# Recurrence chain of a two-layer hybrid decoder step: inverses joined in two column groups, samples and values two at a time, decay folded into the state's rows on GpSimd, fewer operations in VectorE's queue

## The chip, the cores and the metric

The kernel runs on one core of one Trainium2 chip. A core has TensorE (PE in the profile, its weight loads PEld), VectorE (DVE), ScalarE (ACT), GpSimd (POOL), and SyncE (SP), which issues most transfers. The metric is the device time of one execution in microseconds (us); lower is better.

## The reference

One inference step of two layers for a prompt of 512 tokens and 8 decoding samples of one token each, model width 2048. Each layer normalises and modulates its input, multiplies it by one wide matrix, sends one part of the columns through windowed attention (16 heads) and the other through RWKV-7 time mixing (16 heads of 64), gates both, and multiplies by an output matrix. The change touches only the time mixing, whose recurrence is, for each head:

```python
def step(S, inp):
    r_t, w_t, k_t, v_t, kk_t, a_t = inp
    sa = jnp.einsum('bhij,bhj->bhi', S, -kk_t)
    S = (S * w_t[:, :, None, :] + sa[..., None] * (kk_t * a_t)[:, :, None, :]
         + v_t[..., None] * k_t[:, :, None, :])
    return S, jnp.einsum('bhij,bhj->bhi', S, r_t)
```

The 512 prompt tokens start from S = 0, the 8 samples take one step each from a given state.

## The kernel before

**Layout and the large products.** Channels lie on the 128 partitions, the 520 columns (512 tokens and 8 samples) along the free axis. Every product of the input or output matrix is done as three fp32r matmuls per 128x128 block, from a high and a low part of weights and of activations (`quarter`, L370 to L385: `psP`, `psR`, `psQ`, `psA`, `psO` by kind of column tile, 128x260 each). ScalarE makes the high part of a weight block (`hi`, L353), VectorE the low part (`lo`, L363), three blocks ahead of its use.

**Interleaving.** The order on every queue is the order in which the program emits instructions. After each of those large matmuls `Side.tick` runs at most one step of one of the side generators, each of which says with `yield W[n]` how many matmuls are to pass before its next step. So the small work of the recurrence stands in TensorE's queue between large matmuls, at distances that `W` fixes, and in VectorE's, ScalarE's and GpSimd's queues in the same order of emission. Engines work their queues in order; a buffer or a result that is late stops the queue that needs it.

**The chain of one pair of heads.** `chain(p, ...)` (L533 to L842) handles two heads; there are 8 pairs in a layer, 16 in all, and the chain of one pair overlaps with the start of the next. The 512 tokens are cut into 8 chunks of 64, in two groups `g` of four. In order:

- `qk`, `kb` (L603 to L619): queries and keys times decay factors, by VectorE. `rkh` and `rks` (L622, L645; tiles `xhi`, `xlo`) are the two parts of r*k for the bonus term; `bp` (L650) sums them on TensorE.
- `atp` (L634) are the products kb by qk of a chunk; VectorE masks them into `atk` and `atq` (L638), and SyncE writes parts of `atk` to memory (`d1`).
- GpSimd reads them back as `f` (L655) and inverts 32 triangular blocks of 32x32 in 31 steps (L663, L665) into `xi`. During these steps TensorE turns `kb` (`kbT`, L671) and the values (`vT`, L687), ScalarE copies them to `kbt` and to the upper half of `sv`, and `av` (L696) is computed and copied by VectorE to the lower half of `sv` (L701).
- `xi` goes through memory (`d2`) into `xT` (L713), whose unused parts VectorE (L710) and GpSimd (L711) set to zero.
- Two inverses of 32 make one of 64: VectorE turns blocks into `x1` (L721), TensorE multiplies (`t2a`, L726), VectorE copies (L728), TensorE multiplies again (L732), VectorE copies into `xT` (L734). This is done for `g` = 0 and then `g` = 1, 8 products each.
- Eight chunks in sequence (tile `seq`): `rp` (L752) from the state `m0` (tiles `mbd`), `rr` (L753) on VectorE, `sp` (L761), `sv` (L762, L763) on VectorE, `mn` and `yp` (L765 to L768), and the new state by VectorE (L772), which multiplies `mn` by the chunk's decay `pend8` and adds `mp`, the decayed old state made at L756.
- The samples (L785 to L812): `st`, `sa`, `vz` on VectorE, `sab` (L800, L801) on TensorE, then `ys` (L810), one product for each sample, and its copies (L812).

GpSimd also copies the samples' columns (`smp`, L599) early in each chain. Small PSUM tiles come from a ring of four (`ps1`), 128-partition work tiles from a ring of 71 (`t2`). The lines that set the order around the change:

```python
if item[0] <= self.count:
    self.last = self.count
    self.run(item)
```

Of the kernel before, what the change touches and what calls it, by code (L numbers as in the profile page):

```python
# [9 lines left out]
F32 = mybir.dt.float32  # L10
F32R = mybir.dt.float32r
AF = mybir.ActivationFunctionType
ALU = mybir.AluOpType
# [158 lines left out]
def body(ctx, tc, xt, ct, consts, pars, wada, win, wout, lora, sst, swkv, ck, cv, cvn, fing,  # L172
# [324 lines left out]
    def layer(l, hh, hl, xprev, xnext, start, prepare, after):  # L497
# [35 lines left out]
        def chain(p, lw, r, kr, v):  # L533
# [89 lines left out]

            atq, atk = [], []
# [20 lines left out]
            rks = low(rk, rkh)  # L645
# [7 lines left out]
            f = wk.tile([128, 32, 32], F32, tag="inv", name="f", bufs=1)  # L653
            for j in range(4):
                ge.dma_start(out=f[j:128:4], in_=d1.rearrange("b c s t -> (b c) s t"))  # L655
# [5 lines left out]
            for s in range(31):  # L661
# [20 lines left out]
                if s in (15, 25):  # L682
                    g = (s - 5) // 10 - 1
                    ps = ps1("vT").rearrange("p (x t) -> p x t", t=128)
                    for e in range(4):
                        c = 4 * g + e
                        pe.transpose(ps[0:64, e, :], v[:, 64 * c:64 * c + 64], ident)  # L687
                    b = t2([128, 4, 128], "sv")
                    se.copy(out=b[0:64], in_=ps[0:64])
                    sv.append(b)  # L690
                if s == 30:
# [6 lines left out]
                    for g in range(2):  # L698
                        for h in range(2):
                            hs = slice(64 * h, 64 * h + 64)  # L700
                            ve.tensor_copy(sv[g][64:128, :, hs], ps[hs, 4 * g:4 * g + 4])  # L701
                yield W[25] if s < 20 else W[74]
            yield W[26]
            d2 = dp.tile([2, 16, 32, 32], F32, tag="d2", name="d2")
            ge.dma_start(out=d2.rearrange("b c (j i) t -> (b c j) i t", j=4), in_=xi)
            yield W[27]
            xT = []
            for g in range(2):
                a = t2([128, 4, 2, 64], "xT")
                ve.memset(a[0:64], 0.0)  # L710
                ge.memset(a[96:128, :, :, 0:32], 0.0)  # L711
                for b in range(2):
                    ge.dma_start(out=flat(a)[64 + 32 * b:96 + 32 * b, :, 32 * b:32 * b + 32],  # L713
                                 in_=d2[b, 8 * g:8 * g + 8].rearrange("c j t -> j c t"))
                xT.append(a)
            yield W[28]

            x1s, pas = [], []
            for g in range(2):
                x1s.append(sm.tile([128, 8, 32], F32, tag="x1", name="x1", bufs=2))  # L720
                ve.transpose(out=x1s[g][64:96], in_=flat(xT[g])[64:96, :, 0:32])  # L721
            yield W[29]
            for g in range(2):
                pas.append(ps1("t2a").rearrange("p (x t) -> p x t", t=32))
                for e in range(8):
                    pe.matmul(pas[g][96:128, e, :], flat(atk[g])[64:96, e, 32:64], x1s[g][64:96, e, :],  # L726
                              start=True, stop=True)
                ve.tensor_copy(x1s[g][96:128], pas[g][96:128, 0:8])  # L728
                yield W[30]
            for g in range(2):  # L730
                for e in range(8):
                    pe.matmul(pas[g][64:96, 8 + e, :], x1s[g][96:128, e, :], flat(xT[g])[96:128, e, 32:64],  # L732
                              start=True, stop=True)
# [750 lines left out]
```

## Time and profile before

| What | us |
|---|---|
| median of 3 runs | 2412.47 (2407.11 to 2414.36) |
| the profiled execution's own time | 2411.21 |
| its span, first to last instruction | 2409.4 |
| TensorE busy in the span | 2267.3 (94%) |
| VectorE busy | 1540.2 (64%) |
| ScalarE busy | 1031.0 (43%) |
| GpSimd busy | 727.8 (30%) |

The span lies 1.8 us below the profiled execution's own time. In the lines below, a row of instructions has its place in the program, engine, operation, tiles (written before read), shape and count; then busy time in us and the mean duration of one in ns; then how long the engine stood idle just before them and what released it. The view in order of time gives the start and the length in us. The records show an fp32 matmul of the small kind as two records (two passes), a transpose and an fp32r matmul as one. The granted TensorE clock was 0.979 of full speed over the span.

### The profile page before, as it was taken

Reading aid. Unit: us, or ns where it says so; the run is one execution under the profiler, and the core shown is the slowest. Engines: PE = TensorE matmul, PEld = TensorE weight load, DVE = VectorE, ACT = ScalarE, POOL = GpSimd, SP = SyncE. Lnnn points to the kernel's source line nnn. Section 1 sums busy time; section 2 is a strip of 40 time slices with the busy share of each in tenths; the row PEclk is TensorE's granted clock in tenths of the full one; section 3 lists DMA queues with packets and bytes.
Section 4 is the critical chain, followed back from the end, with each engine's and each line's share of the span. In section 5 each row is a group of like instructions: output and inputs, shape, how many; then the busy total and the mean of one; then the engine's idle time right before and its main releaser. Section 6 shows DMA issues by size and latency. Waiting matters only on the chain. (4 is left out here: it accounts for less than half of the span.)

```text
span 2409.4 us, 54300 instructions
## 1 busy us (share of the span) xinstructions
PE 2267.3 (94%) x20900; PEld 2125.9 (88%) x20900; DVE 1540.2 (64%) x3888; ACT 1031.0 (43%) x2250; POOL 727.8 (30%) x1348
## 2 busy tenths in 40 slices
PE   5999999999999999999999999998999999999997
PEld 3899988888889888889989999988989898889997
DVE  3465677777777687543356557677677777865445
ACT  3243344544454456422235335343544445653222
POOL 1106445654366000000012425654565530000112
PEclk8999999999999999999999999999999999999998
DMA  9945555323323224677773455543223332245345
GB/s 343 342 154 173 152 150 159 92 82 94 98 88 90 65 77 127 201 234 248 241 228 88 126 160 167 164 124 98 80 89 94 94 91 63 67 116 148 109 119 176
DMA packets 231396, 338.02 MB, mean 140 GB/s; under 512 B 61761, under 2 KB 82369, under 8 KB 230977
## 3 DMA queue, kind: packets, MB, share of 16 engines
q1 hardware_dynamic: 225248, 321.95, 44.3%
q0 software_dynamic: 5888, 12.59, 1.7%
q8 instruction: 165, 2.70, 0.5%
q14 instruction: 95, 0.77, 0.1%
HBM read 303.97 MB, written 32.56 MB: 140 GB/s over the span
## 5 line engine op out<-in xcount | busy, mean ns | idle before, releaser
L363 DVE TENSOR_TENSOR lo<-raw,hi 128x512 fp32r<-128x512 f32 x568 | 405.2, 714 | 441.1 <-PE psO L378 132.2
L353 ACT CAST hi<-raw 128x512 fp32r<-128x512 f32 x568 | 350.6, 618 | 633.7 <-PE psP L378 219.9
L378 PE MATMUL psP<-hh,hi 128*128 128x260 f32 x1408 | 306.3, 292 | 0.2 <-ACT dm L516 0.2
L378 PE MATMUL psP<-hh,lo 128*128 128x260 f32 x1408 | 306.4, 292 | 0.0
L378 PE MATMUL psP<-hl,hi 128*128 128x260 f32 x1408 | 305.8, 292 | 0.0
L663 POOL TENSOR_TENSOR tmp<-f,xi 128x248 f32<-128x248 f32 (+30 forms) x496 | 260.1, 524 | 81.6 <-DMA f<-d 44.2
L665 POOL TENSOR_TENSOR xi<-xi,tmp 128x248 f32<-128x248 f32 (+30 forms) x496 | 264.0, 532 | 38.9
L378 PEld LDWEIGHTS psP<-hh,hi 128*128 128x128 f32 x1408 | 224.2, 191 | 5.8 <-issue 2.9
L378 PEld LDWEIGHTS psP<-hh,lo 128*128 128x128 f32 x1408 | 224.4, 191 | 5.5 <-issue 3.7
L378 PEld LDWEIGHTS psP<-hl,hi 128*128 128x128 f32 x1408 | 224.5, 191 | 4.6 <-issue 2.5
L378 PE MATMUL psO<-yh,hi 128*128 128x260 f32 x1024 | 223.6, 284 | 3.6 <-DVE xsn L1182 3.6
L378 PE MATMUL psO<-yh,lo 128*128 128x260 f32 x1024 | 223.9, 284 | 1.8 <-DVE lo L363 1.8
L378 PE MATMUL psO<-yl,hi 128*128 128x260 f32 x1024 | 223.4, 284 | 0.0
L378 PEld LDWEIGHTS psO<-yh,hi 128*128 128x128 f32 x1024 | 165.3, 190 | 5.7 <-issue 5.6
L378 PEld LDWEIGHTS psO<-yh,lo 128*128 128x128 f32 x1024 | 165.9, 190 | 3.6 <-DVE lo L363 2.0
L378 PEld LDWEIGHTS psO<-yl,hi 128*128 128x128 f32 x1024 | 165.2, 190 | 1.6 <-issue 1.6
L779 ACT COPY y<-seq 64x64 f32<-64x64 f32 x256 | 52.9, 207 | 262.7 <-DVE mbd L772 215.0
L1319 POOL TENSOR_SCALAR yo<-xnew,fg 128x260 f32<-128x260 f32 x32 | 32.1, 1006 | 404.1 <-DVE xnew L1179 384.4
L443 POOL TENSOR_TENSOR rmsr<-rmsv,mhalf 128x3 f32<-128x3 f32 x6 | 5.6, 940 | 488.4 <-DVE rmsv L440 459.4
L297 PE MATMUL adps<-rawa,cT 128*32 128x128 f32 (+1 forms) x2048 | 116.5, 347 | 26.3 <-DMA rawa<-in_wada_dram 26.1
L378 PE MATMUL psQ<-hl,hi 128*128 128x260 f32 x512 | 116.5, 298 | 0.0
L378 PE MATMUL psQ<-hh,lo 128*128 128x260 f32 x512 | 116.1, 298 | 0.0
(361 smaller groups left out, 5499.5 us busy)
## 6 DMA issues: line engine op xcount, KB each, us to landing
raw<-in_win_dram SPq DMA_DIRECT2D x424, 256.0 KB, 3.3
rawa<-in_wada_dram SPq DMA_DIRECT2D x384, 256.0 KB, 4.8
raw<-in_wout_dram SPq DMA_DIRECT2D x152, 256.0 KB, 3.4
f<-d POOLq DMA_DIRECT2D x64, 128.0 KB, 3.1
gd<-th SPq DMA_DIRECT2D x22, 260.0 KB, 2.3
gr<-gd SPq DMA_DIRECT2D x22, 260.0 KB, 3.7
x<-in_xt_dram SPq DMA_DIRECT2D x16, 260.0 KB, 5.1
yd<-rk SPq DMA_DIRECT2D x16, 260.0 KB, 3.4
```

What stands on the lines that cost most here:

```text
L297: pe.matmul(ap[32 * g:32 * g + 32, 0:w], cT[:, kk, :], raw[g * w // 512][:, c:c + w], start=(kk == 0), stop=(kk == KT - 1))
L353: se.copy(out=his[n], in_=raws[n])
L363: ve.tensor_tensor(out=lo, in0=raws.pop(n), in1=hi, op=ALU.subtract)
L378: pe.matmul(ps[:, h, 0:NH], a[:, k % 4], b[:, h * NH:(h + 1) * NH], start=(k == k0 and j == 0), stop=stop)
L443: ge.tensor_tensor(out=r[:, 0:3], in0=v[:, 0:3], in1=mhalf[:, 0:3], op=ALU.pow)
L663: ge.tensor_tensor(out=tv, in0=f[:, s:s + 1, s + 1:32].to_broadcast([128, 8, 31 - s]), in1=xi[:, :, s:s + 1].to_broadcast([128, 8, 31 - s] ...
L665: ge.tensor_tensor(out=xi[:, :, s + 1:32], in0=xi[:, :, s + 1:32], in1=tv, op=ALU.add)
L779: se.copy(out=y[hs, 64 * c:64 * c + 64], in_=yp[hs, h])
L1319: ge.tensor_scalar(out=out[h][m // 2][:, m % 2], in0=xn[:, h * NH:h * NH + NH], scalar1=fg[:, m:m + 1], scalar2=None, op0=ALU.mult)
```

## The change

Line numbers of the diff are those of the file before; the changed file's numbers are higher by 2 to 9.

```diff
--- before.py
+++ after.py
@@ -621,6 +621,8 @@
             bc = lambda ap: ap.unsqueeze(2).to_broadcast([128, B, 64])
             rkh = high(rk)
 
+            yield W[23] // 2
+            rks = low(rk, rkh)
             atq, atk = [], []
             flat = lambda ap: ap.rearrange("p e h t -> p (e h) t")
             d1 = dp.tile([2, 16, 32, 32], F32, tag="d1", name="d1")
@@ -642,7 +644,6 @@
                 for b in range(2):
                     sy.dma_start(out=d1[b, 8 * g:8 * g + 8].rearrange("c s t -> s c t"),
                                  in_=flat(atk[g])[64 + 32 * b:96 + 32 * b, :, 32 * b:32 * b + 32])
-            rks = low(rk, rkh)
             yield W[23]
             b2 = rk
             for h in range(2):
@@ -651,6 +652,10 @@
                 yield W[24]
 
             f = wk.tile([128, 32, 32], F32, tag="inv", name="f", bufs=1)
+            for g in range(2):
+                b = kb[g].rearrange("p e a t -> p e (a t)")
+                ge.tensor_tensor(out=b, in0=b, in1=pend8[:, 4 * g:4 * g + 4].unsqueeze(2).to_broadcast([128, 4, 128]),
+                                 op=ALU.mult)
             for j in range(4):
                 ge.dma_start(out=f[j:128:4], in_=d1.rearrange("b c s t -> (b c) s t"))
             xi = wk.tile([128, 8, 32], F32, tag="xi", name="xi", bufs=1)
@@ -682,11 +687,12 @@
                 if s in (15, 25):
                     g = (s - 5) // 10 - 1
                     ps = ps1("vT").rearrange("p (x t) -> p x t", t=128)
-                    for e in range(4):
-                        c = 4 * g + e
-                        pe.transpose(ps[0:64, e, :], v[:, 64 * c:64 * c + 64], ident)
+                    for e in range(2):
+                        c = 4 * g + 2 * e
+                        pe.transpose(ps[:, e, :], v[:, 64 * c:64 * c + 128], ident)
                     b = t2([128, 4, 128], "sv")
-                    se.copy(out=b[0:64], in_=ps[0:64])
+                    for e in range(2):
+                        se.copy(out=b[0:64, e:4:2], in_=ps[64 * e:64 * e + 64, 0:2])
                     sv.append(b)
                 if s == 30:
                     ps = ps1("av").rearrange("p (c i) -> p c i", i=64)
@@ -698,41 +704,44 @@
                     for g in range(2):
                         for h in range(2):
                             hs = slice(64 * h, 64 * h + 64)
-                            ve.tensor_copy(sv[g][64:128, :, hs], ps[hs, 4 * g:4 * g + 4])
+                            se.copy(out=sv[g][64:128, :, hs], in_=ps[hs, 4 * g:4 * g + 4])
                 yield W[25] if s < 20 else W[74]
             yield W[26]
+            xT = [t2([128, 4, 2, 64], "xT") for _ in range(2)]
             d2 = dp.tile([2, 16, 32, 32], F32, tag="d2", name="d2")
             ge.dma_start(out=d2.rearrange("b c (j i) t -> (b c j) i t", j=4), in_=xi)
             yield W[27]
-            xT = []
-            for g in range(2):
-                a = t2([128, 4, 2, 64], "xT")
-                ve.memset(a[0:64], 0.0)
+            for a in xT:
+                ge.memset(a[0:64], 0.0)
                 ge.memset(a[96:128, :, :, 0:32], 0.0)
+            for g, a in enumerate(xT):
                 for b in range(2):
                     ge.dma_start(out=flat(a)[64 + 32 * b:96 + 32 * b, :, 32 * b:32 * b + 32],
                                  in_=d2[b, 8 * g:8 * g + 8].rearrange("c j t -> j c t"))
-                xT.append(a)
             yield W[28]
 
-            x1s, pas = [], []
-            for g in range(2):
-                x1s.append(sm.tile([128, 8, 32], F32, tag="x1", name="x1", bufs=2))
-                ve.transpose(out=x1s[g][64:96], in_=flat(xT[g])[64:96, :, 0:32])
+            x1 = sm.tile([128, 2, 8, 32], F32, tag="x1", name="x1", bufs=1)
+            for i in range(2):
+                ve.transpose(out=x1[64:96, i], in_=flat(xT[i])[64:96, :, 0:32])
             yield W[29]
-            for g in range(2):
-                pas.append(ps1("t2a").rearrange("p (x t) -> p x t", t=32))
-                for e in range(8):
-                    pe.matmul(pas[g][96:128, e, :], flat(atk[g])[64:96, e, 32:64], x1s[g][64:96, e, :],
-                              start=True, stop=True)
-                ve.tensor_copy(x1s[g][96:128], pas[g][96:128, 0:8])
-                yield W[30]
-            for g in range(2):
-                for e in range(8):
-                    pe.matmul(pas[g][64:96, 8 + e, :], x1s[g][96:128, e, :], flat(xT[g])[96:128, e, 32:64],
-                              start=True, stop=True)
-                ve.tensor_copy(flat(xT[g])[64:96, :, 32:64], pas[g][64:96, 8:16])
-                yield W[31]
+            pa = ps1("t2a").rearrange("p (x t) -> p x t", t=32)
+            for e in range(8):
+                for i in range(2):
+                    o = (96, 64)[i]
+                    pe.matmul(pa[o:o + 32, e, :], flat(atk[i])[64:96, e, 32:64], x1[64:96, i, e, :], start=True, stop=True)
+            for i in range(2):
+                o = (96, 64)[i]
+                ve.tensor_copy(x1[96:128, i], pa[o:o + 32, 0:8])
+            yield W[30]
+            for e in range(8):
+                for i in range(2):
+                    o = (64, 96)[i]
+                    pe.matmul(pa[o:o + 32, 8 + e, :], x1[96:128, i, e, :], flat(xT[i])[96:128, e, 32:64], start=True,
+                              stop=True)
+            for i in range(2):
+                o = (64, 96)[i]
+                ve.tensor_copy(flat(xT[i])[64:96, :, 32:64], pa[o:o + 32, 8:16])
+            yield W[31]
             y = t2([128, N], "y")
             for c in range(8):
                 if c == 6:
@@ -752,8 +761,6 @@
                     pe.matmul(rp, qk[g][:, e].rearrange("p a t -> p (a t)"), m0, start=True, stop=True)
                     ve.tensor_tensor(out=rr[64:128], in0=rp[64:128], in1=sv[g][64:128, e], op=ALU.add)
                     yield W[32] + 4
-                    mp = sm.tile([128, 128], F32, tag="mp", name="mp", bufs=2)
-                    ve.tensor_scalar(out=mp, in0=m0, scalar1=pend8[:, c:c + 1], scalar2=None, op0=ALU.mult)
                 else:
                     ve.tensor_copy(rr[64:128], sv[g][64:128, e])
                     yield W[32] + 4
@@ -769,11 +776,10 @@
                 for h in range(2):
                     hs = slice(64 * h, 64 * h + 64)
                     if c:
-                        ve.scalar_tensor_tensor(out=m1[hs, hs], in0=mn[hs, hs], scalar=pend8[hs, c:c + 1],
-                                                in1=mp[hs, hs], op0=ALU.mult, op1=ALU.add)
+                        ve.scalar_tensor_tensor(out=m1[hs, hs], in0=m0[hs, hs], scalar=pend8[hs, c:c + 1],
+                                                in1=mn[hs, hs], op0=ALU.mult, op1=ALU.add)
                     else:
-                        ve.tensor_scalar(out=m1[hs, hs], in0=mn[hs, hs], scalar1=pend8[hs, c:c + 1],
-                                         scalar2=None, op0=ALU.mult)
+                        ve.tensor_copy(m1[hs, hs], mn[hs, hs])
                 for h in range(2):
                     hs = slice(64 * h, 64 * h + 64)
                     se.copy(out=y[hs, 64 * c:64 * c + 64], in_=yp[hs, h])
@@ -806,10 +812,13 @@
             sy.dma_start(out=o_ss[l, p], in_=st)
             yield W[38]
             ps = ps1("ys")
-            for b in range(B):
-                pe.matmul(ps[0:64, 2 * b:2 * b + 2], st[:, b], rbd[:, b], start=True, stop=True)
+
+            for b in range(0, B, 2):
+                pe.matmul(ps[:, 2 * b:2 * b + 4], st[:, b:b + 2].rearrange("p b i -> p (b i)"),
+                          rbd[:, b:b + 2].rearrange("p b h -> p (b h)"), start=True, stop=True)
             for h in range(2):
-                ve.tensor_copy(y[64 * h:64 * h + 64, T:N], ps[0:64, h:2 * B:2])
+                for i in range(2):
+                    ve.tensor_copy(y[64 * h:64 * h + 64, T + i:N:2], ps[64 * i:64 * i + 64, 2 * i + h:2 * B:4])
             yield W[39]
 
             yh = high(y)
```

In words: `rks` is made before the products `atp`, not behind them. GpSimd multiplies `kb` by the chunk's decay in place, behind the products `atp` that read it undecayed and ahead of the load of `f`; so `mn` comes out decayed, `mp` is gone, and the new state is one operation on `m0` and `mn`. The values are turned two chunks in one transpose of 128 columns. ScalarE makes the copies from `av`. GpSimd sets all unused parts of `xT` to zero, before the four loads. The two groups' inverses are joined together: one tile `x1`, one PSUM tile `pa`, and 16 products whose neighbours write different 32-column strips of TensorE's array. The samples' last product takes two samples at a time, and four small copies pick out what is wanted. The table `W` is unchanged.

The first place is TensorE's queue at the joining of the fourth pair's inverses in layer 0, before (the first of the four blocks, five rows above, is left out). Names: `t2a` is the PSUM tile, `psP` a large product, `sab` the samples' product; x8 counts matmuls.

```order
L726 MATMUL t2a<-x_6645,atk 32x32 x8
L378 MATMUL psP<-hh,lo 128x260
L378 MATMUL psP<-hh,hi 128x260
L800 MATMUL sab<-sah,sel 128x512
L801 MATMUL sab<-sal,sel 128x512
L378 MATMUL psP<-hh,hi 128x260
L378 MATMUL psP<-hl,hi 128x260 x2
L378 MATMUL psP<-hh,lo 128x260 x2
L732 MATMUL t2a<-xT,x_6643 32x32 x8
L378 MATMUL psP<-hh,hi 128x260 x2
L378 MATMUL psP<-hl,hi 128x260
L732 MATMUL t2a<-xT,x_6645 32x32 x8
```

The same place after the change:

```order
L731 MATMUL t2a<-x_6602,atk 32x32 x16
L378 MATMUL psP<-hl,hi 128x260
L378 MATMUL psP<-hh,lo 128x260 x2
L378 MATMUL psP<-hh,hi 128x260 x2
L378 MATMUL psP<-hl,hi 128x260 x2
L739 MATMUL t2a<-xT,x_6602 32x32 x16
L378 MATMUL psP<-hh,lo 128x260 x2
```

Four blocks of 8 matmuls have become two of 16 with 7 large matmuls between them, and `sab` stands ahead of the first.

The second place is VectorE's queue at the same joining, before; `xlo<-rk` is the low part for the bonus, `rk<-bp,v` its product, `x<-xT` the turned blocks, `x<-t2a` the copies between the two steps, `st` and `sa` the samples.

```order
L411 TENSOR_TENSOR xlo<-rk,xhi 128x520
L363 TENSOR_TENSOR lo<-raw,hi 128x512
L721 STREAM_TRANSPOSE x_6643<-xT 32x256
L721 STREAM_TRANSPOSE x_6645<-xT 32x256
L650 TENSOR_TENSOR rk<-bp,v 128x260 x2
L728 COPY x_6643<-t2a 32x256
L728 COPY x_6645<-t2a 32x256
L363 TENSOR_TENSOR lo<-raw,hi 128x512
L802 TENSOR_TENSOR st<-st,vz 128x512
L803 SCALAR_TENSOR_TENSOR sa<-sab,smp 128x512
L805 TENSOR_TENSOR st<-st,sa 128x512
L734 COPY xT<-t2a 32x8x32 x2
```

And after the change:

```order
L640 TENSOR_TENSOR atk<-atp,cst 128x4x64
L640 TENSOR_TENSOR atq<-atp,cst 128x4x64
L363 TENSOR_TENSOR lo<-raw,hi 128x512
L725 STREAM_TRANSPOSE x_6602<-xT 32x256 x2
L651 TENSOR_TENSOR rk<-bp,v 128x260
L808 TENSOR_TENSOR st<-st,vz 128x512
L809 SCALAR_TENSOR_TENSOR sa<-sab,smp 128x512
L811 TENSOR_TENSOR st<-st,sa 128x512
L651 TENSOR_TENSOR rk<-bp,v 128x260
L363 TENSOR_TENSOR lo<-raw,hi 128x512
L734 COPY x_6602<-t2a 32x256 x2
L743 COPY xT<-t2a 32x8x32 x2
```

The low part `xlo<-rk` has left this place for one ahead of the pair's first `atk`; the three operations on `st` and `sa`, which stood behind the copies `x<-t2a`, now stand ahead of them, with one `rk<-bp,v` and one `lo`.

The third place is GpSimd's queue from the end of the first pair's inversion to the start of the second pair's, before (with buffer numbers: 3042 and 3047 are the two groups' `xT`):

```order
L711 MEMSET xT_3042 32x8x32
L713 DMA xT_3042<-d2_2988 32x8x32 x2
L711 MEMSET xT_3047 32x8x32
L713 DMA xT_3047<-d2_2988 32x8x32 x2
L599 COPY smp_3068<-r_2586 128x8
L599 COPY smp_3068<-rn_3072 128x8
L599 COPY smp_3068<-ta_3124 128x8
L599 COPY smp_3068<-k_3228 128x8
L599 COPY smp_3068<-v_3019 128x8
L655 DMA f_3609<-d1_3377 32x1024 x4
L657 COPY xi_3614<-cst_82 128x256
```

And after the change, from the third of the four settings to zero on (3004 and 3005 are the groups' `xT`):

```order
L715 MEMSET xT_3005 64x512
L716 MEMSET xT_3005 32x8x32
L719 DMA xT_3004<-d2_3006 32x8x32 x2
L719 DMA xT_3005<-d2_3006 32x8x32 x2
L599 COPY smp_3068<-r_2586 128x8
L599 COPY smp_3068<-rn_3072 128x8
L599 COPY smp_3068<-ta_3124 128x8
L599 COPY smp_3068<-k_3228 128x8
L599 COPY smp_3068<-v_3021 128x8
L657 TENSOR_TENSOR kb_3329<-kb_3329,pend_3227 128x512
L657 TENSOR_TENSOR kb_3358<-kb_3358,pend_3227 128x512
L660 DMA f_3621<-d1_3381 32x1024 x4
```

Two products `kb<-kb,pend` stand ahead of the loads of `f`, and four settings of `xT` to zero come in one piece ahead of its four loads.

## The prediction

> **What bounds the kernel now.** I read the page's busy times first, then the view of waits for TensorE, then the timeline around the longest waits.
>
> ```profile
> span 2409.4 us, 54300 instructions
> PE 2267.3 (94%) x20900; PEld 2125.9 (88%) x20900; DVE 1540.2 (64%) x3888; ACT 1031.0 (43%) x2250; POOL 727.8 (30%) x1348
> ```
>
> TensorE is busy for 2267.3 of 2409.4 us, so what leaves its queue leaves the time, and what is left to gain besides is the 142 us in which it stands idle. VectorE at 64% is no bound on the average. The waits of TensorE say where it is one for a while:
>
> ```profile
> PE seq L765 <- DVE sv L763: 20.3, 17, 2.0
> PE bp L418 <- DVE xlo L411: 12.8, 10, 2.5
> PE seq L761 <- DVE rr L753: 10.9, 9, 2.2
> PE t2a L726 <- DVE x L721: 4.1, 4, 1.2
> ```
>
> (us in total, times, the longest.) These 48 us all lie in the chains of the pairs, and VectorE ends all of them. So I count two things: TensorE's own time for the edited blocks, and how VectorE's queue stands where TensorE waits for it. What GpSimd and ScalarE gain or lose counts only if it reaches one of these two.
>
> **TensorE's own time.** The joining of the inverses, one block of 16 records (8 matmuls of two passes):
>
> ```profile
> 258.36 0.28 PE L378 MATMUL psP<-hl,hi 128*128 128x260 f32 x1
> 258.56 0.69 PE L726 MATMUL t2a<-x,atk 32*32 32x32 f32 x16
> 259.18 0.39 PE L378 MATMUL psP<-hl,hi 128*128 128x260 f32 x1
> 259.40 0.28 PE L378 MATMUL psP<-hh,lo 128*128 128x260 f32 x1
> ```
>
> Large matmuls follow each other every 0.12 us, so the next would have started at 258.48; it starts at 259.18, and the one behind it 0.10 late again: 0.80 us for a block. One record lasts 0.19, so the starts lie (0.69 - 0.19) / 15 = 0.033 apart; 16 of them make 0.53, and 0.27 is the price of going into and out of the small tiles. There are 64 such blocks (4 in each of 16 pairs): 51 us. After the change there are 32 blocks of 32 records: the 0.27 is paid half as often, which is 8.6 us. How far apart the records lie when neighbours write different column strips, the trace does not show for 32x32 tiles. Two other products alternate strips:
>
> ```profile
> 221.82 1.15 PE L696 MATMUL av<-sv,atk 64*64 64x64 f32 x32
> 2169.09 0.42 PE L1030 MATMUL ssc<-ktc,qs 64*32 64x129 f32 x8
> L696 PE MATMUL av<-sv,atk 64*64 64x64 f32 x512 | 18.8, 221 | 0.9 <-ACT sv L689 0.8
> L1030 PE MATMUL ssc<-ktc,qs 64*32 64x129 f32 x128 | 6.8, 282 | 4.4 <-DMA ktc<-in_ck_dram 2.9 <-DVE ktc L1023 1.5
> ```
>
> `av` has (1.15 - 0.22) / 31 = 0.030 for 64 columns, less than the 0.033 that 32 columns take in one strip; `ssc` has (0.42 - 0.28) / 7 = 0.020 on four strips. So strips do overlap; the bounds are 0.020 and 0.033 (no overlap at all), and I take 0.024, nearer to `ssc`, since 32 columns in two strips are less work than either. A block is then 0.27 + 32 x 0.024 = 1.04, 32 of them 33 us: **18 us gone** (9 to 22).
>
> The Trainium skill, "TensorEngine Tiling (Array Packing)", section Performance Considerations, warns against tiling a dimension that is already small, since a matmul of one column takes as long as one of 60; and "TensorE: Matmul & The Clock Gate", section "Wait — 56ns, not 53.3ns?", puts the least distance of two starts at about 25 ns. By that figure the blocks would take 34 us, by no overlap 42 us; the 0.020 of `ssc` lies below the page's floor, so the row decides here.
>
> The values and the samples:
>
> ```profile
> 211.79 0.60 PE L687 MATMUL vT<-cst,v 128*64 128x128 f32 x4
> 212.15 0.49 PE L378 MATMUL psP<-hl,hi 128*128 128x260 f32 x2
> 212.47 0.40 PE L378 MATMUL psP<-hh,lo 128*128 128x260 f32 x2
> 212.71 0.28 PE L378 MATMUL psP<-hh,hi 128*128 128x260 f32 x1
> 338.70 0.40 PE L378 MATMUL psP<-hh,lo 128*128 128x260 f32 x2
> 339.03 1.09 PE L810 MATMUL ys<-rbd,st 128*64 128x2 f32 x16
> 340.06 0.51 PE L378 MATMUL psP<-hh,hi 128*128 128x260 f32 x2
> 340.40 0.40 PE L378 MATMUL psP<-hl,hi 128*128 128x260 f32 x2
> 2376.05 0.61 PE L435 MATMUL rms<-one,acc 128*128 128x1 f32 x4
> ```
>
> From 211.79 to 212.71 there are four transposes and four large matmuls: 0.92 - 0.48 = 0.44, 0.11 a transpose. Two fewer in each of 32 blocks: **7 us gone**. The samples' block costs 340.06 - 338.94 + 0.10 = 1.22. After the change it has 8 records with 128 columns of weights and 4 of data, like `rms`, whose four records of 0.29 lie (0.61 - 0.29) / 3 = 0.107 apart: 0.86, with 0.1 for the way out 0.96. 16 times 0.26 is **4 us** (0 to 6).
>
> **The waits.** In most pairs VectorE runs without a gap up to the copies `sv`, and TensorE stands for two microseconds:
>
> ```profile
> 545.18 0.58 DVE L772 SCALAR_TENSOR_TENSOR mbd<-seq,pend,mp 64x64 f32<-64x64 f32 x2
> 545.92 1.03 DVE L710 MEMSET xT<- 64x512 f32 x2 [0.16 <-issue]
> ...
> 551.68 0.17 DVE L1103 TENSOR_SCALAR gsa<-th 128x8 f32<-128x8 f32 x1
> 551.76 0.28 DVE L756 TENSOR_SCALAR mp<-mbd,pend 128x128 f32<-128x128 f32 x1
> 552.30 0.23 DVE L763 COPY sv<-seq 64x64 f32<-64x64 f32 x1
> 552.58 0.49 PE L765 MATMUL seq<-sv,kbt 128*128 128x128 f32 x2 [2.01 <-DVE sv L763]
> ```
>
> The settings to zero (1.03) and `mp` (0.28) go from just this stretch: 1.3 us of a wait of 2.0. Waits of this size stand in about 10 of the 16 pairs (17 waits of `sv`, 9 of `rr`): 10 x 1.2 = **12 us** (5 to 18). What is late next is the rest of VectorE's work there, 0.7 us.
>
> The wait for `xlo` (12.8) goes whole, since `rks` now stands ahead of the masks: **13 us**. VectorE may then wait for ScalarE's `xhi` there, and does so at the cost of its next wait, for `atp`, which it has already:
>
> ```profile
> DVE atk L638 <- PE atp L634: 22.3, 27, 2.2
> L411 DVE TENSOR_TENSOR xlo<-rk,xhi 128x520 fp32r<-128x520 f32 x16 | 11.1, 695 | 0.5 <-POOL smp L599 0.4
> ```
>
> **The new wait.** Where the inverses are joined, TensorE used to work on group 1 while VectorE copied group 0. Now both copies `x<-t2a` stand between the two blocks, which lie 7 large matmuls apart: 0.84 us. The copies alone take two times 0.43. And the order has moved: in 10 of the 16 pairs three operations on the samples, with one `rk<-bp,v` or a `lo`, now stand between the turned blocks and the copies.
>
> ```profile
> L803 DVE SCALAR_TENSOR_TENSOR sa<-sab,smp 128x512 f32<-128x512 f32 x16 | 11.0, 689 | 1.3 <-PE sab L801 1.0
> L728 DVE COPY x<-t2a 32x256 f32<-32x256 f32 x32 | 13.8, 430 | 12.8 <-PE t2a L726 12.1
> ```
>
> From the moment that `x1` is ready, VectorE needs about 0.4 + 3 x 0.69 + 0.4 + 0.8 = 3.7 us until both copies are done; TensorE, if it had waited for `x1`, is back after 1.04 + 0.84 + 0.1 = 2.0: it stands for 1.7. Where it came later than `x1` it stands less. I take 1.6 in 10 pairs and 0.4 in the others, 18 us, and 2 us for the second turned block that the first matmuls now need: **20 us given back** (5 to 35).
>
> **What costs nothing.** GpSimd's two products per pair run while it waits for `atk` to come back from memory, 16.8 us a pair:
>
> ```profile
> L655 POOL DMA_DIRECT2D f<-d x64 | 34.1, 538 | 269.2 <-DMA d<-atk 269.2
> L472 POOL TENSOR_TENSOR xn<-x,rstd 128x512 f32<-128x512 f32 x4 | 5.1, 1278 | 36.9 <-PE adps L297 23.9 <-issue 7.2 <-DVE hl L492 5.8
> L713 POOL DMA_DIRECT2D xT<-d x64 | 38.1, 600 | 40.9 <-DMA d<-xi 38.7 <-DVE mp L756 2.2
> ```
>
> They take 2 x 1.28. The settings to zero lie in the 2.4 us per pair for which the loads of `xT` wait for `xi`; without that cover they would delay `xT` by 1 us. ScalarE gets 64 copies and the halves of 32: at most 0.58 each by `sv<-vT`, some 40 us on an engine that waits far longer for TensorE.
>
> ```profile
> L689 ACT COPY sv<-vT 64x512 f32<-64x512 f32 x32 | 18.5, 580 | 21.6 <-PE vT L687 21.4
> L353 ACT CAST hi<-raw 128x512 fp32r<-128x512 f32 x568 | 350.6, 618 | 633.7 <-PE psP L378 219.9
> ```
>
> **The sum.** -18 - 7 - 4 - 12 - 13 + 20 = -34 us, against the profiled execution's own 2411.2 us: **2377 us**, 1.4% below; the median of the runs is 1.3 us above that execution, inside their spread.
>
> **The rivals.**
> 1. The column strips do not overlap (0.033 stays): 9 us less gain, 2386. `av` speaks against it; that no 32x32 block of this trace alternates strips speaks for it. 0.13.
> 2. The join costs nothing: VectorE, which loses 112 `mp` of 0.28 and 32 settings of 0.5 us (47 us) and the copies of `av`, has caught up before it. 20 us more gain, 2357. Against it: the waits of up to 2.5 us for `xlo` show VectorE late just ahead of the join. 0.17.
> 3. The join costs its upper bound, and the waits of `seq` only move: -18 - 7 - 4 - 5 - 13 + 35 = -12, 2399. 0.10.
> 4. Slower: GpSimd's products hold VectorE up. VectorE's subtraction takes 0.70 us as `xlo<-rk`, when GpSimd waits, and 0.84 as `xlo<-y`, during GpSimd's steps of 0.5. If each of 32 products of 1.28 us stops VectorE for its length, 41 us come into the stretch ahead of the join, which TensorE then waits for: 2377 + 41 = 2418. It decides from 34 / 32 = 1.06 us per product on. For it: the products start when `atp` is done, with VectorE's masks; against it: the masks read PSUM, and the subtraction lost 0.14, less than one step. 0.08.
>
> ```profile
> L411 DVE TENSOR_TENSOR xlo<-y,xhi 128x520 fp32r<-128x520 f32 x32 | 26.9, 840 | 0.5
> ```
>
> The Trainium skill, "SBUF — State Buffer", section "SBUF: two separate sides", says that a GpSimd operation and a VectorE operation with two SBUF inputs exclude each other for a whole instruction. By it rival 4's price is paid once per product that meets such an operation; the 0.14 us above agrees in kind, and no run here shows it for a long product.
>
> **How the numbers follow.** The forecast has 0.52, the rivals 0.13, 0.17, 0.10 and 0.08. The bounds of the terms give -22 - 8 - 6 - 18 - 13 + 5 = -62 (2349) and -9 - 6 - 0 - 5 - 10 + 35 = +5 (2416); both ends at once are unlikely, and I leave a tenth out on each side: 2353 to 2403. Faster by over 0.3% (7 us, about what a measurement of this kernel tells from no change) is the forecast, rivals 1 and 2 and most of 3: 0.88. Within 0.3%: 0.06. Slower by more: 0.06, nearly all of it rival 4.
>
> **What would show it.** `t2a` blocks of 1.04 us mean strips that overlap, 1.3 that they do not. `bp` must be gone from TensorE's waits, `sv` down to about 10 us in total, and a new wait must stand at the second `t2a` block, for VectorE's copies, of about 18 us. Rival 4 would show in `lo`, `r` and `sa` longer than 1 us right behind `atp`. The prediction is wrong if the waits do not fall where VectorE's work went, or if the join costs more than the blocks gain.

## The result, and the profile after

| | before | after |
|---|---|---|
| median | 2413.28 us (2407.11 to 2414.36, 4 runs) | 2345.07 us (2339.24 to 2348.35, 4 runs) |
| profiled execution, span | 2409.4 us | 2343.1 us |
| TensorE busy / idle in the span | 2267.3 / 142.1 us | 2220.5 / 122.6 us |

The ratio is 0.9713, with a 95% interval of 0.9692 to 0.9734: 68 us, 2.8% faster. The forecast was 2377 us (2353 to 2403), a gain of 34: the sign was right, the size half of what came. One run of a kernel below, that with TensorE's parts alone, took 11889 us, five times its others; it is in none of the medians and ratios. The page after begins so:

```profile
span 2343.1 us, 53879 instructions
PE 2220.5 (95%) x20708; PEld 2094.3 (89%) x20708; DVE 1482.1 (63%) x3712; ACT 1057.8 (45%) x2346; POOL 790.9 (34%) x1412
```

Of the 66 us that the span lost, 47 are TensorE's busy time and 19.5 its idle time. TensorE's waits in the pairs after, from the same list and in the same columns as before (waits elsewhere in the layer are left out, here and in the lists below):

```profile
PE t2a L739 <- DVE x L734: 14.2, 9, 2.2
PE seq L772 <- DVE sv L770: 12.2, 12, 1.6
PE seq L761 <- DVE mbd L779: 5.8, 6, 1.1
PE t2a L731 <- DVE x L725: 3.4, 3, 1.3
PE seq L768 <- issue: 1.2, 3, 0.7
```

The waits of `bp` and of `rr` are gone (at the product that waited for `rr`, now L768, 1.2 us are left) and `sv` fell from 20.3 to 12.2; the wait at the second joined block is there, with 14.2 us, as the prediction said it would be. The edited blocks of TensorE, from the timeline (start, length, and so on, as above):

```profile
258.90 0.28 PE L378 MATMUL psP<-hl,hi 128*128 128x260 f32 x1
259.12 0.69 PE L739 MATMUL t2a<-xT,x 32*32 32x32 f32 x32
259.74 0.39 PE L378 MATMUL psP<-hl,hi 128*128 128x260 f32 x1
259.97 0.40 PE L378 MATMUL psP<-hh,lo 128*128 128x260 f32 x2
...
333.32 0.28 PE L378 MATMUL psP<-hh,lo 128*128 128x260 f32 x1
333.44 0.95 PE L817 MATMUL ys<-rbd,st 128*128 128x4 f32 x8
334.25 0.37 PE L378 MATMUL psP<-hh,lo 128*128 128x260 f32 x1
334.46 0.40 PE L378 MATMUL psP<-hh,hi 128*128 128x260 f32 x2
```

A joined block of 32 records lasts 0.69 us: as long as a block of 16 did. From 258.90 to 259.74 are 0.84 us, of which the large matmul itself takes 0.12, and the second large matmul behind the block comes 0.11 late again. So a joined block costs 0.82 us, as much as a block of 16 cost (0.82 is the median of the blocks between undisturbed large matmuls, in both kernels). The samples' block costs 0.90 where by the same measure it cost 1.22.

### The profile page after: what moved, and what is told of

The parts are those of the page before. It is cut to its first block, busy times and chain, and to the rows that moved or that the text cites. A ratio compares the mean times of both kernels' runs of the same rounds, so it can differ in the third digit from the quotient of the medians.

```text
span 2343.1 us, 53879 instructions
## 1 busy us (share of the span) xinstructions
PE 2220.5 (95%) x20708; PEld 2094.3 (89%) x20708; DVE 1482.1 (63%) x3712; ACT 1057.8 (45%) x2346; POOL 790.9 (34%) x1412
## 4 chain that ended last, share of the span: by engine, by line
PE 71%; DVE 12%; DMA 6%; ACT 4%; issue 3%; POOL 3%; SPq 1%; DVEq 0%; ACTq 0%; POOLq 0%
PE psP L378 17%; PE psO L378 14%; PE psA L378 6%; PE psR L378 6%; PE psQ L378 5%; PE psS L378 4%; PE adps L297 4%; DMA rawa<-in_wada_dram 2%; DVE lo L363 2%; PE psK L378 2%; POOL xi L670 1%; PE atp L636 1%; POOL tmp L668 1%; PE seq L772 1%; DMA raw<-in_wout_dram 1%
## 5 line engine op out<-in xcount | busy, mean ns | idle before, releaser
L363 DVE TENSOR_TENSOR lo<-raw,hi 128x512 fp32r<-128x512 f32 x568 | 414.0, 730 | 454.3 <-PE psO L378 133.5
L670 POOL TENSOR_TENSOR xi<-xi,tmp 128x248 f32<-128x248 f32 (+30 forms) x496 | 283.5, 572 | 38.9
L297 PEld LDWEIGHTS adps<-rawa,cT 128*32 128x32 f32 x2048 | 55.2, 114 | 67.2 <-DMA rawa<-in_wada_dram 23.1
```

The source lines that it names most:

```text
L297: pe.matmul(ap[32 * g:32 * g + 32, 0:w], cT[:, kk, :], raw[g * w // 512][:, c:c + w], start=(kk == 0), stop=(kk == KT - 1))
L363: ve.tensor_tensor(out=lo, in0=raws.pop(n), in1=hi, op=ALU.subtract)
L670: ge.tensor_tensor(out=xi[:, :, s + 1:32], in0=xi[:, :, s + 1:32], in1=tv, op=ALU.add)
```

## The experiments

Every kernel was timed against the kernel before on its own chip; the ratios are to be compared with 0.9713. One thousandth is 2.4 us, and two such ratios tell some 8 us apart. Four questions: what is the join worth on TensorE, what are the two halves of the change worth alone, where does VectorE's lateness go, and what do GpSimd's products cost.

**The order of the strips.** The joined blocks as in the changed kernel, with the two loops exchanged in both:

```diff
-            for e in range(8):
-                for i in range(2):
+            for i in range(2):
+                for e in range(8):
```

> The changed kernel, but in each of the two joined blocks the eight products of group 0 stand ahead of the eight of group 1, so that sixteen records in a row write the same column strip. Theory A (two strips overlap wholly, so that 32 records cost what 16 did): the overlap is lost, 16 more records of 0.033 us count in each of 32 blocks, 17 us; the blocks are 1.2 us long in the timeline instead of 0.69, the time is about 2362 us, 0.9783 of before. Theory B (the gain of the join is that the entry into small tiles is paid half as often, and the order of strips does nothing): blocks and time stay as they are, 0.971.

Measured: 0.9755 (0.9729 to 0.9781), 2350 us, 10 us above the changed kernel. A block with one strip at a time, in the timeline:

```profile
343.20 1.09 PE L731 MATMUL t2a<-x,atk 32*32 32x32 f32 x32
```

1.09 against 0.69: 0.40 us in each of 32 blocks, 13 us, of which the shorter wait at the second block (10.8 us in place of 14.2) gives 3 back. Theory A's mechanism holds; its 17 us were 10, since the blocks grew by 0.40 us and not by the 0.53 of sixteen records at 0.033, and since a wait fell. It says more than the prediction dared: the records of two strips lie (0.69 - 0.19) / 31 = 0.016 us apart, those of one strip (1.09 - 0.19) / 31 = 0.029. The second strip costs nothing.

**Four blocks again.** The changed kernel with the lines of the join as they were before, with two tiles `x1`, two PSUM tiles, and yields of 7, 7, 3 and 3 ticks. Of the first step:

```diff
-            for e in range(8):
-                for i in range(2):
-                    o = (96, 64)[i]
-                    pe.matmul(pa[o:o + 32, e, :], flat(atk[i])[64:96, e, 32:64], x1[64:96, i, e, :], start=True, stop=True)
...
+            for g in range(2):
+                pas.append(ps1("t2a").rearrange("p (x t) -> p x t", t=32))
+                for e in range(8):
+                    pe.matmul(pas[g][96:128, e, :], flat(atk[g])[64:96, e, 32:64], x1s[g][64:96, e, :],
+                              start=True, stop=True)
```

> The changed kernel with the inverses joined as before, in four blocks of eight products a pair, and everything else of the change kept. Theory A (a joined block costs 0.80 us as a block of 16 records did, so the join takes 64 - 32 times 0.80 = 26 us off TensorE): 26 come back and the wait of 14 us at the second joined block goes, 12 us above the changed kernel, 0.976 of before. Theory C (the joined block costs 1.04 us as predicted, and what the prediction missed lies with VectorE): 18 come back and 14 go, 4 us above, 0.973. Theory D (the joining wait is in truth free, since TensorE would stand as long for something else): 26 us above, 0.982.

Measured: 0.9807 (0.9783 to 0.9832), 2365 us: 23 us above the changed kernel. Theory D's 0.982 lies in the interval, A's 0.976 and C's 0.973 lie outside it. TensorE's waits in this kernel:

```profile
PE seq L764 <- DVE rr L758: 9.3, 11, 1.6
PE t2a L731 <- DVE x L726: 8.1, 8, 1.9
PE seq L768 <- DVE sv L766: 7.5, 9, 1.5
PE seq L757 <- DVE mbd L775: 1.1, 3, 0.6
```

There is no wait between the blocks, but one for `rr` of 9.3 us and one of 8.1 ahead of the first block; with the joined blocks these two nearly go (1.2 and 3.4), 14.2 us come at the second block, and `sv` and `mbd` grow from 8.6 to 18.0. In all, the pairs' waits are 26 us here and 37 after, so the join gives back 11 us of its 23. By the waits some 15 us would come back (26 - 11), and the profiled execution, with a span of 2356.6 us, has 13.5. But it is the fastest of the six, and the medians say 23. So where some 8 us of the 23 lie stays open.

**Each half alone.** TensorE's three parts alone (the joined blocks, values and samples two at a time) and the four parts that relieve VectorE alone. The first is the changed kernel with the four parts put back that are undone one by one further down; the second has its four blocks as above, and the lines of before for `vT` and `ys`.

> The changed kernel without the four parts that relieve VectorE: the low part of rk stands behind the masks again, the decay is VectorE's (mp, no products on GpSimd), the zeros of xT and the copies of av are VectorE's. Left are the joined blocks, the values and the samples two at a time. Theory A: TensorE's own time falls by 26 + 7 + 3 = 36 us, the wait at the second joined block is 14 to 25 us, so 11 to 22 us gain, 0.991 to 0.995 of before. Theory C (blocks of 1.04 us, and a wait of 20): 28 - 20 = 8 us, 0.997.

> The changed kernel with TensorE's three parts undone: four blocks of eight products, four transposes of the values, eight products of the samples. Left are the four parts that relieve VectorE. By the waits of the two traces: bp 13 us and the waits of seq 20 us gone, 33 us, 0.986 of before (theory A: TensorE's waits say all that the relief is worth). Theory C (the relief is worth more than TensorE's waits say, since stalls lie within its busy time): 45 us or more, 0.981 or less. As predicted from the profile of before: 25 us, 0.990.

Measured: TensorE's parts alone 0.9809 (0.9783 to 0.9835), 43 us below before at the medians of 2365.36 and 2408.84; VectorE's parts alone 0.9845 (0.9810 to 0.9881), 35 us. Together the halves make 78 where the whole makes 68; with intervals of 5 to 9 us on each of the three, the 10 between them can't be told from nothing. VectorE's half came out as its waits said (theory A, 33 us); the 25 of the prediction lie outside the interval. For TensorE's half both theories missed, and the half that I had priced at 9 us of net gain (29 off TensorE, 20 given back) made 43: here the prediction failed. The waits of TensorE's parts alone:

```profile
PE seq L769 <- DVE sv L767: 18.1, 15, 2.3
PE bp L418 <- DVE xlo L411: 16.4, 10, 2.5
PE seq L756 <- DVE mbd L776: 7.7, 13, 1.2
PE t2a L734 <- DVE x L729: 6.9, 8, 1.5
PE seq L765 <- DVE rr L757: 2.2, 6, 0.6
PE t2a L726 <- DVE x L720: 1.2, 1, 1.2
```

Before, these two waits of the pairs stood beside the four that the prediction shows:

```profile
PE seq L752 <- DVE mbd L772: 7.7, 11, 1.4
PE t2a L726 <- ACT hi L353: 1.5, 2, 0.8
```

The wait at the second block is 6.9 us, though VectorE has all its old work. At the same time `bp` waits longer than before (16.4) and `rr` hardly at all (2.2 against 10.9). In all, the pairs' waits fall from 57 to 52 us: on top of the old kernel the join costs nothing in waits. With 26 us off TensorE for the joined blocks, 7 for the values and 5 for the samples, these 5 make the 43. In VectorE's half `bp` is gone from the list, and `rr` and `sv` are lower:

```profile
PE seq L763 <- DVE rr L757: 8.8, 10, 1.6
PE seq L767 <- DVE sv L765: 6.7, 9, 1.6
```

**The low part of `rk` behind the masks again.** This changes the order of VectorE's queue, not its work.

```diff
-            yield W[23] // 2
-            rks = low(rk, rkh)
...
+            rks = low(rk, rkh)
             yield W[23]
```

> The changed kernel with the low part of rk computed behind the masks again. As predicted: the wait of bp for xlo comes back whole, 13 us above the changed kernel, 0.977 of before. Theory B (VectorE's lateness is paid once, where TensorE first needs it): the wait of bp comes back, but the wait at the second joined block, some 12 us of the program later in the same pair's chain, falls by the same, 0.971.

Measured: 0.9724 (0.9704 to 0.9745): 3 us above the changed kernel, which it can't be told from. Three of the waits:

```profile
PE bp L418 <- DVE xlo L411: 18.8, 10, 2.5
PE seq L771 <- DVE sv L769: 8.7, 11, 1.4
PE t2a L738 <- DVE x L733: 6.4, 10, 1.0
```

`bp` waits 18.8 us again, and the join 6.4 in place of 14.2, `sv` 8.7 in place of 12.2. Theory B holds. The timeline of before shows why: `bp` and the first block of another pair's join lie 3 us apart, and the wait at `bp` is the time in which VectorE catches up.

```profile
419.30 0.28 PE L418 MATMUL bp<-xhi,sel 128*128 128x260 f32 x1
421.36 0.39 PE L418 MATMUL bp<-xlo,sel 128*128 128x260 f32 x1 [1.77 <-DVE xlo L411]
...
424.55 0.69 PE L726 MATMUL t2a<-x,atk 32*32 32x32 f32 x16
```

**More ticks, and copies on ScalarE.** Two ways to take away the wait at the second block: 14 more ticks between the blocks, which also puts three operations on the samples behind the copies, and the copies themselves on another engine (first those of the first block, then those of both).

```diff
-                ve.tensor_copy(x1[96:128, i], pa[o:o + 32, 0:8])
-            yield W[30]
+                se.copy(out=x1[96:128, i], in_=pa[o:o + 32, 0:8])
+            yield W[30]
```

> The changed kernel with 14 more ticks of the other stream's matmuls between the two joined blocks (21 in place of 7). In the order of instructions the three operations on the samples then stand behind VectorE's copies of the first block, no longer ahead of them. Theory A (the wait of 14 us at the second joined block is the join's own price, and behind 7 of these 9 waits TensorE runs at half its clock for some 3 us, 1.5 us each): the wait goes and the stretches with it, 14 + 10 = 24 us below the changed kernel, 0.961 of before. Theory B (VectorE is late there in any case, and TensorE pays for it wherever it next needs VectorE): the wait goes, those of seq for rr and sv grow from 13 us to some 25, the time stays, 0.971.

> The changed kernel with the two copies of the first joined block on ScalarE in place of VectorE. Theory A (what stands ahead of these copies in VectorE's queue makes TensorE wait): the wait falls from 14 us to 5 or less, 10 to 20 us below the changed kernel, 0.963 to 0.967 of before. Theory B (VectorE's lateness is paid elsewhere): 0.971. A third way: ScalarE's queue holds casts that wait for later matmuls of the other stream, the wait is as long for ScalarE as it was for VectorE: 0.971 with the wait in the list under ScalarE's name.

> The changed kernel with the copies of both joined blocks on ScalarE. With those of the first alone it was 0.9642 of before. If the copies of the second hold VectorE up in the sequence that follows: 14 us less in VectorE's queue, of which the waits of seq (20 us) give back some 5: 0.962. If ScalarE is late instead, the wait of seq for rr and xT grows: 0.966 or above.

Measured: more ticks 0.9684 (0.9660 to 0.9709), 2336 us; the first copies on ScalarE 0.9642 (0.9616 to 0.9667), 2329 us; all four 0.9627 (0.9613 to 0.9641), **2323 us**, the best kernel of this study, 1% below the changed one. The waits with more ticks, then with the first copies on ScalarE:

```profile
PE seq L768 <- DVE rr L762: 14.4, 11, 1.9
PE t2a L731 <- DVE x L725: 7.1, 8, 1.7
PE seq L772 <- DVE sv L770: 6.4, 10, 1.9
PE av L702 <- ACT sv L695: 4.6, 5, 1.2
```

```profile
PE seq L772 <- DVE sv L770: 12.8, 12, 1.6
PE t2a L731 <- DVE x L725: 6.6, 7, 1.7
PE seq L761 <- DVE mbd L779: 6.1, 6, 1.3
PE t2a L739 <- ACT x L734: 2.9, 2, 1.6
```

With more ticks the wait at the second block is gone from the list, and `rr` (14.4) and the first block (7.1) have it instead, with `sv` down from 12.2 to 6.4 and a new wait at `av` for ScalarE: VectorE has the same work, and its lateness mostly changes its place; theory B, but for some 7 us that are at the edge of what can be told. With the copies on ScalarE 32 operations of 0.43 us, 14 us of work, leave VectorE. Of the 14.2 us at the second block 2.9 stay, the first block's wait grows by 3, and theory A holds. The run takes away two things at once, 14 us of VectorE's work and the place of the copies behind the operations on the samples, and doesn't part them. The other two copies, again 14 us of work, add 3.5 us, which the intervals don't tell from nothing.

**VectorE's relief, part by part.** The changed kernel with one part undone each: the decay (`mp`) on VectorE again, without GpSimd's products; the zeros of `xT`; the copies of `av`.

```diff
-            for g in range(2):
-                b = kb[g].rearrange("p e a t -> p e (a t)")
-                ge.tensor_tensor(out=b, in0=b, in1=pend8[:, 4 * g:4 * g + 4].unsqueeze(2).to_broadcast([128, 4, 128]),
-                                 op=ALU.mult)
...
+                    ve.tensor_scalar(out=mp, in0=m0, scalar1=pend8[:, c:c + 1], scalar2=None, op0=ALU.mult)
```

```diff
-                ge.memset(a[0:64], 0.0)
+                ve.memset(a[0:64], 0.0)
```

```diff
-                            se.copy(out=sv[g][64:128, :, hs], in_=ps[hs, 4 * g:4 * g + 4])
+                            ve.tensor_copy(sv[g][64:128, :, hs], ps[hs, 4 * g:4 * g + 4])
```

> The changed kernel with the decay as before: mp on VectorE (112 of 0.28 us), no products on GpSimd. As predicted: 0.28 us of VectorE's gapless stretch in about 10 pairs, 3 us above the changed kernel, 0.9725 of before. Theory A (all seven mp of a pair lie in or ahead of waits for rr, sv and mbd, and what of them isn't hidden counts): a third to two thirds of 31 us, 10 to 20 us above, 0.976 to 0.980. If TensorE's waits for VectorE say nothing of it (they are saturated by the join): 0.971.

> The changed kernel with the zeros of xT set by VectorE (two of 0.5 us a pair) as before. As predicted: 1.03 us in VectorE's gapless stretch of about 10 pairs, 9 to 10 us above the changed kernel, 0.975 of before. If GpSimd's settings had themselves a price (they stand ahead of the loads of xT): 0.971 or below.

> The changed kernel with the four copies of av a pair on VectorE as before (64 of 0.43 us). As predicted: nothing is waited for there, 0.971 of before. Theory A (all of VectorE's work between the masks and the sequence counts once it runs without a gap): 4 x 0.43 us in the pairs that wait, some 10 of 16, 17 us, 0.978.

Measured: decay 0.9734 (0.9708 to 0.9760), 5 us above the changed kernel; zeros 0.9763 (0.9749 to 0.9777), 12 us; copies of `av` 0.9746 (0.9720 to 0.9771), 8 us. With the 3 us of the low part these make 28, and all four together 23 (0.9809 against 0.9713). The zeros are as predicted (10), with `sv` at 19.6 us in place of 12.2:

```profile
PE seq L772 <- DVE sv L770: 19.6, 13, 2.3
```

The decay too, within its interval; that of `av` had been priced at nothing and is at the edge of what can be told: in its profiled execution, the fastest of its five, the span is 2341.3 us, no longer than after, so where its 8 us lie stays open.

**GpSimd's products twice.** The two products of a pair are done a second time, into the memory of `f`, which the loads right behind them overwrite.

```diff
+            for g in range(2):
+                b = kb[g].rearrange("p e a t -> p e (a t)")
+                spare = f.rearrange("p a t -> p (a t)")[:, 512 * g:512 * g + 512].rearrange("p (e x) -> p e x", e=4)
+                ge.tensor_tensor(out=spare, in0=b, in1=pend8[:, 4 * g:4 * g + 4].unsqueeze(2).to_broadcast([128, 4, 128]),
+                                 op=ALU.mult)
             for j in range(4):
```

> The changed kernel with GpSimd's two products of kb and the decay done a second time, into memory that the load of f overwrites right behind. The prediction's rival 4 (GpSimd's products hold VectorE up, 1.28 us each): 32 more of them cost 41 us, 0.988 of before. Its forecast (they lie in GpSimd's wait for atk): nothing, 0.971; the lo, r and mask operations of VectorE keep their mean.

Measured: 0.9816 (0.9792 to 0.9839), 2368 us: 25 us above the changed kernel, 0.8 us a product. Neither theory gave this number, but rival 4's mechanism is there. First the changed kernel's two groups of operations on the samples, then the same two with the products doubled:

```profile
L793 DVE TENSOR_TENSOR sa<-st,smp 128x512 f32<-128x512 f32 x16 | 11.8, 736 | 0.0
L797 DVE TENSOR_TENSOR st<-st,smp 128x512 f32<-128x512 f32 x16 | 11.0, 685 | 0.1
```

```profile
L802 DVE TENSOR_TENSOR st<-st,smp 128x512 f32<-128x512 f32 x16 | 16.0, 999 | 0.1
L798 DVE TENSOR_TENSOR sa<-st,smp 128x512 f32<-128x512 f32 x16 | 15.2, 948 | 0.0
```

These operations grow by 0.2 to 0.3 us each and VectorE's busy time by 20 us (1482.1 to 1502.6); TensorE's waits for the two joined blocks go from 3.4 and 14.2 to 13.1 and 18.0. A later end of the inversion is not the way: VectorE stands idle for the transfer of `xT` for 3.0 us in all, 1.9 in the changed kernel.

The changed kernel itself has such meetings: beside 18 of its 32 products stands an operation of VectorE with both inputs in SBUF (16 `lo`, one `xlo`, one `sa`) that takes 0.94 to 1.54 us in place of 0.69, and each of the 18 ends 0.55 or 0.56 us after the product. The clearest, at 329 us, first VectorE's subtraction, then GpSimd's product, and behind them a usual one, with the product first:

```profile
329.20 1.54 DVE L411 TENSOR_TENSOR xlo<-rk,xhi 128x520 fp32r<-128x520 f32 x1
...
328.65 1.53 POOL L657 TENSOR_TENSOR kb<-kb,pend 128x512 f32<-128x512 f32 x1 [6.22 <-PE atp L636]
```

```profile
1303.95 1.04 POOL L657 TENSOR_TENSOR kb<-kb,pend 128x512 f32<-128x512 f32 x1 [3.58 <-PE atp L636]
...
1304.54 1.00 DVE L363 TENSOR_TENSOR lo<-raw,hi 128x512 fp32r<-128x512 f32 x1
```

The subtraction takes 1.54 us where it usually takes 0.70 (median), and ends 0.56 after the product: it waited for it. So the price of a product depends on what VectorE does beside it. As the change places them, 30 of the 32 products run beside a mask, which reads PSUM and keeps its 0.42 us, and the 18 meetings lengthen VectorE's work by some 7 us in all (the whole part is a gain of 5 us); a second pair of products right behind costs 25. This agrees with the Trainium skill, "SBUF — State Buffer", section "SBUF: two separate sides": the exclusion is per whole instruction, and of VectorE's operations it meets those with two inputs from SBUF and those in a two-port mode, of which no run here shows the second.

## Why the prediction was half right

| term | predicted | traces before and after |
|---|---|---|
| joined blocks, TensorE's own time | -18 | -26 (64 blocks of 0.82 to 32 of 0.82) |
| values, samples | -7, -4 | -7, -5 |
| waits of `seq` | -12 | -20 (38.9 to 19.2 us, with `mbd`) |
| wait of `bp` | -13 | -13 |
| waits at the joined blocks | +20 | +12 (5.6 to 17.6) |
| sum | -34 | -59 |

- **The step that failed** is "20 us given back" as a term beside "the wait for `xlo` goes whole". I priced each wait by itself and added them. But one engine's lateness is one quantity. TensorE pays it at the first place where it needs VectorE, and is then in step for the next. `bp` without its wait makes a longer wait at the join (14.2 with the move, 6.4 without: 8 us of the join's wait belong to it, and in the changed kernel the move is worth 3 us, which can't be told from nothing, not 13); the join's wait in turn takes the place of that for `rr`, 10.9 us before and 2.2 with TensorE's parts alone. The join's price in waits, priced at 20, was -5 on top of the old kernel (57 to 52 us) and +11 on top of VectorE's relief (26 to 37). The rival "the join costs nothing" was nearer, with 2357, and still 12 us off.
- **The size of the overlap.** The term of the joined blocks was 8 us too small: a block was to cost 1.04 us and costs 0.82. The strips overlap wholly. The spacing is 0.016, below the 0.020 that I took for the lowest bound from `ssc`, whose four strips each carry 129 columns. The bound was a row of another shape, not a bound.
- **`seq`.** The two operations named (zeros, `mp`) cost 12 and 5 us when put back one by one, 17 where 12 were predicted; the join alone takes 11 more from these waits (38.9 to 28.0), and the two overlap.
- **What is left.** 66 - 59 = 7 us lie outside these terms. Two things are known of it: the list of waits shows each some 0.16 us too short (at `bp` above, the last matmul starts at 419.30 and the next would have started at 419.42, so 1.94 us are lost where 1.77 are shown), and there are 94 waits in place of 112: 3 us; and stretches at half the clock, told below, are 61.4 us in place of 68.3: at most 3 us. The rest is within the rounding of the terms.
- **The rest of the working held**: values, samples, zeros, `mp`, and ScalarE's new copies, which stand in none of TensorE's waits after. The wait for `xlo` went as predicted, but not its 13 us. GpSimd's products, put at nothing, lengthen VectorE's work by the 7 us told above.

## What to carry to other kernels

Waits of one engine for another are not terms to be added: ask how much work the late engine has up to a point, and count a wait once, at the first place where it is met. Moving an operation within a late engine's queue bought next to nothing here (3 us for 13 of a wait removed). What taking work off it buys hangs on the place: about its length twice (12 us for 16 of zeros, 17 for the first 14 of copies), far less three times (5 for 31 of `mp`, 8 for 28 of `av`, 3.5 for the other 14 of copies). That the difference is slack behind the operation is likely, and was not tried by itself. And a small matmul block should be priced by its strips: two of 32 columns cost what one does.

## What the runs showed of the hardware beside this

**Half the clock stands behind many long waits of TensorE.** The large matmuls behind some waits lie 0.22 us apart in place of 0.12. The view of windows of the changed kernel around the wait of 1.61 us at 487.59 (stretch, its length, busy times of the five engines, granted clock, ...):

```profile
484.80:486.50 1.70, 1.19 (x17) 0.93 (x11) 1.67 (x4) 0.00 (x0) 0.00 (x0) 1.00 0.27 63
486.50:488.50 2.00, 0.91 (x34) 0.87 (x35) 1.16 (x4) 0.00 (x0) 1.81 (x4) 1.00 0.61 188
488.50:489.10 0.60, 0.60 (x7) 0.60 (x7) 0.59 (x2) 0.00 (x0) 0.60 (x2) 0.92 0.84 160
489.10:491.90 2.80, 2.80 (x15) 2.80 (x15) 1.02 (x4) 1.22 (x3) 0.20 (x1) 0.50 0.66 211
```

The granted clock falls to 0.50 some 1.4 us after the wait has ended, and by the trace's record of the clock it stays there for 3.4 us, to 492.4. Of the 2.8 us of the last row some 1.4 are lost, which the profile books as busy time. Over the 14 profiled executions of this study, from 60 us after the start to 80 us before the end, that record has 176 such stretches, each of 3.4 us or two to four times as long; 165 of them begin during a wait of 1 us or more, or within 2.5 us of its end. A stretch begins so at 54 of 77 waits of 2 us and more, 80 of 174 between 1.5 and 2, 35 of 233 between 1 and 1.5, and 23 of 732 shorter ones. That the wait is the cause was not tried by itself. The Trainium skill, "TensorE: Matmul & The Clock Gate", section "What's actually happening", has the same half clock after an idle window of about 3.4 us; here waits of half that length go before it.

If the wait is the cause, one wait of 2 us is worse than four of 0.5. The times agree with it: the stretches sum to 61.4 us in the changed kernel, 37.5 with the first copies on ScalarE and 85.3 with GpSimd's products doubled, and with the same 20708 matmul records TensorE's busy time is 6.9 us shorter and 11.6 longer than in the changed kernel. So this is likely a part of why those copies gained 17 us where the wait at the second block fell by 11 and that at the first grew by 3, and of why the products cost 25 where the waits at the two blocks grew by 13.5.
